# Chunked state-space scan on one core: the state product placed behind the D products, and two low-part subtractions on VectorE instead of GpSimd

## The chip, the cores and the metric

The kernel runs on one core of one Trainium2 chip. The metric is the device time of one execution in microseconds, and less is better. The kernel before takes 2060.54 us, the median of three runs (2057.94, 2060.54 and 2061.54 us).

## What is computed

One layer of a streaming encoder over 1024 tokens of width 1024, in float32: RMSNorm, a mixer of two branches (a gated linear recurrence, and a Mamba-2 state-space scan), a gated merge, an output projection with residual, then RMSNorm, SwiGLU with residual, and a last RMSNorm. The change touches the state-space scan alone. Cut to what matters (heads in 4 groups of 8, head width 64, state 128):

```python
def ssd_scan(x, dt, A, Bm, Cm):
    xdt = (x * dt[..., None])
    a_cs = jnp.cumsum(dt * A, axis=2)                      # within a chunk
    decay = jnp.exp(where(causal, a_cs_l - a_cs_s, -inf))
    scores = einsum('bclgn,bcsgn->bclsg', Cc, Bc)
    y_diag = einsum('bclsg,bclsgk,bcsgkp->bclgkp', scores, decay, xdt)
    decay_to_end = jnp.exp(a_cs[:, :, -1:] - a_cs)
    states = einsum('bclgn,bclgk,bclgkp->bcgkpn', Bc, decay_to_end, xdt)
    # h[c+1] = h[c] * exp(a_cs[c, -1]) + states[c]
    y_off = einsum('bclgn,bcgkpn,bclgk->bclgkp', Cc, prev, jnp.exp(a_cs))
    return y_diag + y_off
# then y + D*x, times silu(z), a group norm, and the branch's weights
```

## The kernel before

The kernel goes through its stages one after the other: first norm and input projections, the recurrence, the scan, the branch weights, the merge and output projection, then the feed-forward part. Most products are in "f32r" with three terms: an operand is split into a high part (a copy by ScalarE) and a low part (the operand less its high part, one subtraction), and high×high, high×low and low×high are added up in one PSUM bank.

The scan runs over 4 head groups and in each over 8 chunks of 128 tokens, 32 chunks in all. For each chunk:

- `chunk_in` (lines 784 to 813): TensorE computes the scores of the chunk and the transpose of B into one "aux" bank (L790, L792), and the transposes of x into the bank "turn" (L795). VectorE makes `xdt` (L802). GpSimd weights it by the decay to the chunk's end, `xwf` (L806); ScalarE copies the high part into `xw` (L808); **GpSimd makes the low part (L809)**. VectorE also makes `xd`, D times x (L811), and multiplies the decays `ed` by the scores (L812).
- `gate_z` (L145): 24 products of z for a chunk further on, which depend on nothing in the scan. They need a free bank among 4 ("mm"), which a SiLU on ScalarE (L772) empties.
- `chunk_out` (from L816): `py`, the old state's part of y, 3 products (L825, from `state_hl`); **`pst`, the state's product, 3 products (L829, from `b_tm` and `xw`)**; **`pd`, the D products, one for each of 8 heads (L832, from `ed` and `xdt`; each shows as two records in the profile)**. Then GpSimd decays the old state (L840), VectorE adds the new part (L841), ScalarE copies its high part (L843) and **GpSimd makes its low part `state_hl` (L844)** for the next chunk's `py`. VectorE scales `py` into `yo` (L848), GpSimd adds it to `xd` (L850), VectorE adds `pd` (L851), GpSimd multiplies by SiLU(z) (L853), ScalarE squares for the norm (L854).
- `chunk_ed` prepares the decays of a later chunk: a load (L778), a subtraction on VectorE (L779), a mask on GpSimd (L781), an exponential on ScalarE (L903).

Four PSUM banks go to z, one to the transposes of x, and three ("aux") are handed round among the scores, `py`, `pst` and `pd`, in the order in which the code asks for them. At the borders between groups VectorE also splits the next group's weights `wz` (L83), four 128x1024 subtractions, and computes a small reciprocal root (L163 to L174).

The order in which each engine's instructions stand is not that of the code: the kernel is built under a scheduler (the last lines of the file ask for it) that reorders instructions by its own estimates. So a change of two lines and one moved block gives a new order on all five engines, and the order is fixed at build: an engine does not pass over an instruction that waits.

Of the kernel before, what the change touches and what calls it, by code (L numbers as in the profile page):

```python
# [13 lines left out]
ALU = mybir.AluOpType  # L14
# [8 lines left out]
HG = 8  # L23
# [9 lines left out]
def hybrid_block_kernel(  # L33
# [6 lines left out]
    nc = tc.nc  # L40
    x, out = x[0], out[0]
# [18 lines left out]
    def bank(tag="aux"):  # L60
        t = psum.tile([P, 512], F32, name=tag, tag=tag, bufs=BANKS[tag])
        return t

    def f32(t):
        return t.bitcast(F32)
# [91 lines left out]
    def flat(t):  # L157
        return t.rearrange("p a b -> p (a b)")
# [50 lines left out]
    def evac(hi, lo, pv):  # L209
        nc.scalar.copy(out=hi, in_=pv)  # L210
        nc.vector.tensor_tensor(out=lo, in0=pv, in1=f32(hi), op=ALU.subtract)
# [496 lines left out]
    with phase("ssd") as pp:  # L708
# [76 lines left out]
        def chunk_in(g, c, b_ch, c_ch, xs_ch, ed):  # L785
            h0 = g * HG
            hs = slice(h0, h0 + HG)
            cs = slice(c * P, (c + 1) * P)
            pt = bank()
            nc.tensor.matmul(pt[:, :P], b_ch[:, cs], c_ch[:, cs], start=True, stop=True)  # L790
            if c < NC - 1:
                nc.tensor.transpose(out=pt[:, P:2 * P], in_=b_ch[:, cs], identity=ident)  # L792
            px = bank("turn")
            for i in range(4):
                nc.tensor.transpose(out=px[:, i * P:(i + 1) * P], in_=xs_ch[i][:, cs], identity=ident)  # L795
            b_tm = None
            if c < NC - 1:
                b_tm = pp.tile([P, 2, P], F32R, name="b_tm", tag="b_tm", bufs=1)
                evac(b_tm[:, 0, :], b_tm[:, 1, :], pt[:, P:2 * P])
            pxv = px.rearrange("p (h d) -> p h d", d=64)  # L800
            xdt = pp.tile([P, HG, 64], F32, name="xdt", tag="xdt", bufs=2)
            nc.vector.tensor_tensor(out=xdt, in0=pxv, in1=bcast(dt_t[:, c, hs], 64), op=ALU.mult)  # L802
            xw = None
            if c < NC - 1:
                xwf = pp.tile([P, HG, 64], F32, name="xwf", tag="tmp", bufs=1)
                nc.gpsimd.tensor_tensor(out=xwf, in0=xdt, in1=bcast(dte_t[:, c, hs], 64), op=ALU.mult)  # L806
                xw = pp.tile([P, 2, GC], F32R, name="xw", tag="xw", bufs=1)
                nc.scalar.copy(out=xw[:, 0, :], in_=flat(xwf))  # L808
                nc.gpsimd.tensor_tensor(out=xw[:, 1, :], in0=flat(xwf), in1=f32(xw[:, 0, :]), op=ALU.subtract)  # L809
            xd = pp.tile([P, HG, 64], F32, name="xd", tag="xd", bufs=3)  # L810
            nc.vector.tensor_tensor(out=xd, in0=pxv, in1=bcast(d_bc[:, hs], 64), op=ALU.mult)  # L811
            nc.vector.tensor_tensor(out=ed, in0=ed, in1=pt[:, :P].unsqueeze(1).broadcast_to([P, HG, P]), op=ALU.mult)  # L812
            return ed, xdt, xw, xd, b_tm
# [3 lines left out]
        def chunk_out(g, c, c_hl, parts, state, sz):  # L817
            ed, xdt, xw, xd, b_tm = parts
# [3 lines left out]
            if c > 0:  # L822
                py = bank()
                for q, (i, j) in enumerate(((0, 0), (0, 1), (1, 0))):
                    nc.tensor.matmul(py, c_hl[:, i, cs], state[1][:, j, :], start=(q == 0), stop=(q == 2))  # L825
            if c < NC - 1:
                pst = bank()
                for q, (i, j) in enumerate(((0, 0), (0, 1), (1, 0))):
                    nc.tensor.matmul(pst, b_tm[:, i, :], xw[:, j, :], start=(q == 0), stop=(q == 2))  # L829
            pd = bank()  # L830
            for h in range(HG):
                nc.tensor.matmul(pd[:, h * 64:(h + 1) * 64], ed[:, h, :], xdt[:, h, :], start=True, stop=True)  # L832
            if c < NC - 1:
                psv = pst.rearrange("p (h d) -> p h d", d=64)
                if c == 0:
                    new = pp.tile([P, HG, 64], F32, name="state", tag="state", bufs=1)
                    nc.vector.tensor_copy(out=new, in_=psv)
                else:
                    new = state[0]
                    nc.gpsimd.tensor_tensor(out=new, in0=new, in1=bcast(dec_t[:, c, hs], 64), op=ALU.mult)  # L840
                    nc.vector.tensor_tensor(out=new, in0=psv, in1=new, op=ALU.add)  # L841
                parts = pp.tile([P, 2, GC], F32R, name="state_hl", tag="state_hl", bufs=1)
                nc.scalar.copy(out=parts[:, 0, :], in_=flat(new))  # L843
                nc.gpsimd.tensor_tensor(out=parts[:, 1, :], in0=flat(new), in1=f32(parts[:, 0, :]), op=ALU.subtract)  # L844
                state = new, parts
            if c > 0:
                yo = pp.tile([P, HG, 64], F32, name="yo", tag="tmp", bufs=1)
                nc.vector.tensor_tensor(out=yo, in0=py.rearrange("p (h d) -> p h d", d=64),  # L848
                                        in1=bcast(eacs_t[:, c, hs], 64), op=ALU.mult)
# [29 lines left out]
        for g in range(NG):  # L879
# [11 lines left out]
            for c in range(NC):  # L891
                parts = chunk_in(g, c, b_ch, c_ch, xs_ch, eds.pop(0))
# [399 lines left out]
    with phase("ffn_out", "right") as pp:  # L1292
# [3 lines left out]
        for f0, nk, wf in pieces:  # L1296
            last = f0 + nk == NFT
            for c in range(NC):
# [22 lines left out]
                if last:  # L1321
# [4 lines left out]
                    for n in range(2):  # L1326
# [3 lines left out]
                        else:  # L1330
                            nc.vector.scalar_tensor_tensor(out=o[:, ns], in0=hres[c][:, ns], scalar=r[:, 0:1],
                                                           in1=g_bc[:, ns], op0=ALU.mult, op1=ALU.mult)
# [33 lines left out]
```

## Time and profile before

| what | us |
|---|---|
| median of three runs | 2060.54 |
| the profiled execution, its own time | 2063.49 |
| its span, from first to last instruction | 2061.7 |
| the window of the scan, 685 to 1030 us of the span | 345 |
| TensorE busy in that window | 316.25 |
| VectorE busy | 251.35 |
| GpSimd busy | 268.50 |
| ScalarE busy | 210.50 |

PE is TensorE's products, PEld its weight loads (they overlap with products), DVE is VectorE, ACT ScalarE, POOL GpSimd, SP the engine that issues most DMAs. "busy" is the time in which an instruction of that engine was under way. On VectorE and GpSimd it includes time in which the instruction has started and is held up by the other of the two. PEclk is the granted TensorE clock as a share of full speed. The profiled execution is 2.95 us above the median.

### The profile page before, as it was taken

Reading aid. Unit: us, or ns where it says so; the run is one execution under the profiler, and the core shown is the slowest. Engines: PE = TensorE matmul, PEld = TensorE weight load, DVE = VectorE, ACT = ScalarE, POOL = GpSimd, SP = SyncE. Lnnn points to the kernel's source line nnn. Section 1 sums busy time; section 2 is a strip of 40 time slices with the busy share of each in tenths; the row PEclk is TensorE's granted clock in tenths of the full one; section 3 lists DMA queues with packets and bytes.
Section 4 is the critical chain, followed back from the end, with each engine's and each line's share of the span. In section 5 each row is a group of like instructions: output and inputs, shape, how many; then the busy total and the mean of one; then the engine's idle time right before and its main releaser. Section 6 shows DMA issues by size and latency. Waiting matters only on the chain.

```text
span 2061.7 us, 23665 instructions
## 1 busy us (share of the span) xinstructions
PE 1975.0 (96%) x8972; PEld 1625.1 (79%) x8972; DVE 1300.8 (63%) x1600; ACT 933.3 (45%) x1329; POOL 721.0 (35%) x470
## 2 busy tenths in 40 slices
PE   5999999999999998998899999998999999999998
PEld 4777877878787887877688888876888888888887
DVE  7787877866675667777546455468555545545445
ACT  5555465567776556666322213334333233342112
POOL 4554544420010688787600030026433433213000
PEclk9999999999999999998899999999999999999999
DMA  5534443442212543442233253521232232255212
GB/s 171 148 104 117 124 122 107 123 133 64 62 54 82 199 144 108 165 157 92 77 103 122 94 172 114 204 82 62 72 103 75 75 96 82 82 186 192 82 62 82
DMA packets 201558, 231.57 MB, mean 112 GB/s; under 512 B 11148, under 2 KB 154980, under 8 KB 201444
## 3 DMA queue, kind: packets, MB, share of 16 engines
q1 hardware_dynamic: 201444, 230.06, 34.8%
q8 instruction: 71, 1.16, 0.2%
q14 instruction: 43, 0.35, 0.1%
HBM read 174.32 MB, written 55.71 MB: 112 GB/s over the span
## 4 chain that ended last, share of the span: by engine, by line
PE 76%; DVE 10%; ACT 4%; POOL 4%; issue 3%; DMA 2%; SPq 0%; DVEq 0%; POOLq 0%; ACTq 0%
PE mm L315 32%; PE mm L134 17%; PE mm L145 15%; PE aux L145 6%; DVE conv L444 2%; DVE wc L83 2%; PE aux L832 2%; DMA w_raw<-in_w_in_dram 1%; POOL xd L853 1%; PE aux L677 1%; POOL xw L809 1%; PE aux L829 1%; POOL state_hl L844 1%; DVE slot L1167 1%; POOL xwf L806 1%
## 5 line engine op out<-in xcount | busy, mean ns | idle before, releaser
L315 PE MATMUL mm<-slot,wc 128*128 128x512 f32 x2376 | 552.9, 391 | 6.1 <-DVE slot L1167 5.0
L315 PEld LDWEIGHTS mm<-slot,wc 128*128 128x128 f32 x2376 | 447.5, 189 | 102.9 <-DVE slot L1167 6.3
L315 PE MATMUL mm<-t,wc 128*128 128x512 f32 x960 | 230.4, 396 | 11.5 <-DVE rows L469 10.0
L315 PEld LDWEIGHTS mm<-t,wc 128*128 128x128 f32 x960 | 182.7, 191 | 53.1 <-DVE rows L469 12.6
L134 PE MATMUL mm<-slot,w_hi 128*128 128x512 f32 x704 | 218.1, 390 | 0.0
L145 PE MATMUL mm<-slot,slot 128*128 128x512 f32 (+1 forms) x924 | 213.0, 387 | 0.0
L145 PE MATMUL mm<-wz,slot 128*128 128x512 f32 x768 | 200.3, 407 | 5.8 <-ACT sz L772 3.8
L145 PEld LDWEIGHTS mm<-slot,slot 128*128 128x128 f32 x924 | 171.6, 188 | 34.9
L83 DVE TENSOR_TENSOR wc<-s,wc 128x512 fp32r<-128x512 f32 x168 | 168.6, 1033 | 32.8 <-ACT wc L82 32.8
L145 PEld LDWEIGHTS mm<-wz,slot 128*128 128x128 f32 x768 | 143.8, 193 | 37.3 <-ACT sz L772 4.7
L134 PEld LDWEIGHTS mm<-slot,w_hi 128*128 128x128 f32 x704 | 132.0, 188 | 27.9 <-DVE dt_rows L617 0.3
L134 PE MATMUL mm<-slot,w_lo 128*128 128x512 f32 x352 | 137.1, 389 | 0.0
L145 PE MATMUL aux<-slot,slot 128*128 128x512 f32 x528 | 124.4, 389 | 0.0
L444 DVE SCALAR_TENSOR_TENSOR conv<-rows,par,conv 128x1023 f32<-128x1023 f32 (+2 forms) x72 | 115.4, 1607 | 4.6 <-ACT conv L440 4.5
L145 PEld LDWEIGHTS aux<-slot,slot 128*128 128x128 f32 x528 | 99.1, 188 | 20.6
L1103 POOL TENSOR_TENSOR u_u<-u_u,e 128x512 f32<-128x512 f32 x22 | 28.6, 1300 | 246.0 <-DVE u_u L1097 246.0
L82 ACT CAST slot<-w_raw 128x1024 fp32r<-128x1024 f32 x44 | 46.0, 1052 | 141.3 <-PE mm L145 52.6
L82 ACT CAST wc<-s 128x512 fp32r<-128x512 f32 x168 | 98.0, 617 | 10.6 <-POOL s L430 4.8
L82 ACT CAST w_hi<-w_raw 128x1024 fp32r<-128x1024 f32 x36 | 37.7, 1050 | 136.2 <-PE mm L134 133.3
L488 POOL TENSOR_TENSOR rows<-rows,e 128x512 f32<-128x512 f32 x20 | 41.3, 2067 | 162.9 <-DVE rows L477 95.0
L83 DVE TENSOR_TENSOR slot<-w_raw,slot 128x1024 fp32r<-128x1024 f32 x44 | 57.4, 1310 | 52.4 <-ACT slot L82 52.3
L982 POOL TENSOR_TENSOR acc<-acc,gt 128x1024 f32<-128x1024 f32 x8 | 20.6, 2583 | 187.9 <-DMA gt<-g_dram 187.9
(291 smaller groups left out, 3535.8 us busy)
## 6 DMA issues: line engine op xcount, KB each, us to landing
w_raw<-in_w_in_dram SPq DMA_DIRECT2D x60, 512.0 KB, 4.6
ed<-acs_dram SPq DMA_DIRECT2D x32, 512.0 KB, 3.8
xbc_dram<-conv SPq DMA_DIRECT2D x24, 512.0 KB, 2.7
w_raw<-in_w_branch_dram SPq DMA_DIRECT2D x24, 512.0 KB, 3.6
w_raw<-in_w_ffn_in_dram SPq DMA_DIRECT2D x22, 512.0 KB, 4.4
raw_pair<-in_w_ffn_in_dram SPq DMA_DIRECT2D x22, 512.0 KB, 4.5
act_dram<-act SPq DMA_DIRECT2D x22, 512.0 KB, 2.7
act_raw<-act_dram SPq DMA_DIRECT2D x22, 512.0 KB, 3.5
```

Of the source, the lines that this page charges most:

```text
L82: nc.scalar.copy(out=hi, in_=src)
L83: nc.vector.tensor_tensor(out=lo, in0=src, in1=f32(hi), op=ALU.subtract)
L134: nc.tensor.matmul(ps[:m, :], ww[:, k, :], xx(p, k, h), start=(k == 0 and i == 0), stop=(k == nk - 1 and i == 2))
L145: nc.tensor.matmul(ps, xx(p, k), ww(q, k), start=(k == 0 and i == 0), stop=(k == nk - 1 and i == 2))
L315: nc.tensor.matmul(ps, w[:, k, :], x[q][:, k, :], start=(start and k == 0 and i == 0), stop=(k == 3 and i == 2), skip_group_check=True)
L444: nc.vector.scalar_tensor_tensor(out=t[:, d:], in0=x[:, :S - d], scalar=tap[j], in1=t[:, d:], op0=ALU.mult, op1=ALU.add)
L488: nc.gpsimd.tensor_tensor(out=d["hi"][:, half(1)], in0=d["hi"][:, half(1)], in1=d["e5"], op=ALU.add)
L677: nc.tensor.matmul(pg, w[:, j, :], uu[:, hs], start=(q == 0), stop=(q == 2))
L806: nc.gpsimd.tensor_tensor(out=xwf, in0=xdt, in1=bcast(dte_t[:, c, hs], 64), op=ALU.mult)
L809: nc.gpsimd.tensor_tensor(out=xw[:, 1, :], in0=flat(xwf), in1=f32(xw[:, 0, :]), op=ALU.subtract)
L832: nc.tensor.matmul(pd[:, h * 64:(h + 1) * 64], ed[:, h, :], xdt[:, h, :], start=True, stop=True)
L1103: nc.gpsimd.tensor_tensor(out=d["u3"], in0=d["u3"], in1=d["e5"], op=ALU.add)
```

## The change

In `chunk_in` the low part of `xw` and in `chunk_out` the low part of `state_hl` are computed by VectorE instead of GpSimd: same operands, same shape (128x512, float32 from SBUF in, f32r out). In `chunk_out` the block that issues `pd` stands ahead of the one that issues `pst`. The products are the same ones. Line numbers of the changed file differ in two places: there the D products are L828 and the state product is L832.

```diff
                 nc.scalar.copy(out=xw[:, 0, :], in_=flat(xwf))
-                nc.gpsimd.tensor_tensor(out=xw[:, 1, :], in0=flat(xwf), in1=f32(xw[:, 0, :]), op=ALU.subtract)
+                nc.vector.tensor_tensor(out=xw[:, 1, :], in0=flat(xwf), in1=f32(xw[:, 0, :]), op=ALU.subtract)
...
+            pd = bank()
+            for h in range(HG):
+                nc.tensor.matmul(pd[:, h * 64:(h + 1) * 64], ed[:, h, :], xdt[:, h, :], start=True, stop=True)
             if c < NC - 1:
                 pst = bank()
                 for q, (i, j) in enumerate(((0, 0), (0, 1), (1, 0))):
                     nc.tensor.matmul(pst, b_tm[:, i, :], xw[:, j, :], start=(q == 0), stop=(q == 2))
-            pd = bank()
-            for h in range(HG):
-                nc.tensor.matmul(pd[:, h * 64:(h + 1) * 64], ed[:, h, :], xdt[:, h, :], start=True, stop=True)
...
                 nc.scalar.copy(out=parts[:, 0, :], in_=flat(new))
-                nc.gpsimd.tensor_tensor(out=parts[:, 1, :], in0=flat(new), in1=f32(parts[:, 0, :]), op=ALU.subtract)
+                nc.vector.tensor_tensor(out=parts[:, 1, :], in0=flat(new), in1=f32(parts[:, 0, :]), op=ALU.subtract)
```

What the scheduler makes of it, at two places. First TensorE, at a chunk in the middle of a group, before (`turn` holds the transposes of x; `xw`, `b_tm` go into the state product, `xdt`, `ed` into the D products):

```order
L795 MATMUL turn<-ident,xs_6200 128x128
L829 MATMUL aux<-xw,b_tm 128x512 x3
L832 MATMUL aux<-xdt,ed 128x64 x8
L790 MATMUL aux<-c_ch,b_ch 128x128
L792 MATMUL aux<-ident,b_ch 128x128
```

and in the changed kernel, at a chunk of the same kind:

```order
L795 MATMUL turn<-ident,xs_5501 128x128
L825 MATMUL aux<-state_hl,c_hl 128x512
L828 MATMUL aux<-xdt,ed 128x64 x8
L832 MATMUL aux<-xw,b_tm 128x512 x3
```

What was the transposes, the state product, the D products is now the transposes, the old state's product, the D products, the state product. At 28 of the 32 chunks there is a state product, and in the changed order it never stands ahead of all D products of its chunk.

Second VectorE, one chunk in the middle of the third group, before:

```order
L211 TENSOR_TENSOR b_tm<-aux,b_tm 128x128
L812 TENSOR_TENSOR ed<-ed,aux 128x1024
L779 TENSOR_TENSOR ed<-ed,acs_t 128x1024
L848 TENSOR_TENSOR yo<-aux,eacs_t 128x512
L841 TENSOR_TENSOR state<-aux,state 128x512
L851 TENSOR_TENSOR xd<-aux,xd 128x512
L802 TENSOR_TENSOR xdt<-turn,dt_t 128x512
L811 TENSOR_TENSOR xd<-turn,d_bc 128x512
```

and in the changed kernel:

```order
L211 TENSOR_TENSOR b_tm<-aux,b_tm 128x128
L812 TENSOR_TENSOR ed<-ed,aux 128x1024
L848 TENSOR_TENSOR yo<-aux,eacs_t 128x512
L851 TENSOR_TENSOR xd<-aux,xd 128x512
L802 TENSOR_TENSOR xdt<-turn,dt_t 128x512
L811 TENSOR_TENSOR xd<-turn,d_bc 128x512
L841 TENSOR_TENSOR state<-aux,state 128x512
L211 TENSOR_TENSOR b_tm<-aux,b_tm 128x128
L812 TENSOR_TENSOR ed<-ed,aux 128x1024
L809 TENSOR_TENSOR xw<-xwf,xw 128x512
L779 TENSOR_TENSOR ed<-ed,acs_t 128x1024
L844 TENSOR_TENSOR state_hl<-state,state_hl 128x512
```

The two subtractions (L809, L844) have joined VectorE's queue, and the addition of the state (L841), which stood between `yo` and the addition of `pd` (L851), now stands behind the next chunk's `xdt` and `xd`: L851 follows L848 directly. On GpSimd 28 instructions of L809 and 28 of L844 are gone from the queue. In SP's queue the loads of `ed` and the stores of `y_dram` change places with each other and with some loads. Outside the scan the orders are the same.

## Rows read from the trace of the kernel before

**Rows 1.** The page, its span and part 1.

```profile
span 2061.7 us, 23665 instructions
PE 1975.0 (96%) x8972; PEld 1625.1 (79%) x8972; DVE 1300.8 (63%) x1600; ACT 933.3 (45%) x1329; POOL 721.0 (35%) x470
```

**Rows 2.** Busy time by engine, the window of the scan; columns in the first row.

```profile
core 0: us, PE busy (x) PEld busy (x) DVE busy (x) ACT busy (x) POOL busy (x), PEclk, DMA share, GB/s
685.00:1030.00 345.00, 316.25 (x1644) 263.50 (x1643) 251.35 (x330) 210.50 (x298) 268.50 (x200) 0.93 0.38 126
```

**Rows 3.** The same view by stretches of 20 us, four of them.

```profile
780.00:800.00 20.00, 15.84 (x79) 11.80 (x79) 17.64 (x24) 12.65 (x18) 17.02 (x12) 1.00 0.53 159
...
820.00:840.00 20.00, 20.00 (x113) 17.09 (x112) 11.21 (x15) 14.14 (x20) 17.96 (x15) 1.00 0.51 184
...
860.00:880.00 20.00, 16.57 (x81) 12.76 (x80) 19.08 (x30) 13.67 (x18) 14.57 (x11) 0.97 0.46 145
...
1000.00:1020.00 20.00, 14.89 (x58) 11.62 (x57) 9.62 (x13) 4.52 (x9) 12.19 (x11) 0.66 0.17 53
```

**Rows 4.** PE's groups, 680 to 1030 us: busy, mean, idle before, releasers.

```profile
L145 PE MATMUL mm<-wz,slot 128*128 128x512 f32 x663 | 175.7, 409 | 5.8 <-ACT sz L772 3.8 <-DVE wz L83 1.1 <-ACT wz L82 0.9
...
L829 PE MATMUL aux<-xw,b_tm 128*128 128x512 f32 x84 | 32.8, 452 | 9.9 <-ACT xw L808 6.0 <-POOL xw L809 3.8
L825 PE MATMUL aux<-state_hl,c_hl 128*128 128x512 f32 x84 | 31.8, 435 | 3.5 <-ACT state_hl L843 2.6 <-POOL state_hl L844 0.8
```

**Rows 5.** PE in order of time, the five longest waits of the state product.

```profile
798.96 0.73 PE L829 MATMUL aux<-xw,b_tm 128*128 128x512 f32 x2 [2.28 <-POOL xw L809]
...
878.26 0.50 PE L829 MATMUL aux<-xw,b_tm 128*128 128x512 f32 x1 [1.98 <-ACT xw L808]
...
963.27 0.50 PE L829 MATMUL aux<-xw,b_tm 128*128 128x512 f32 x1 [2.30 <-ACT xw L808]
...
997.76 0.72 PE L829 MATMUL aux<-xw,b_tm 128*128 128x512 f32 x2 [0.95 <-POOL xw L809]
...
1005.39 0.80 PE L829 MATMUL aux<-xw,b_tm 128*128 128x512 f32 x1 [1.15 <-ACT xw L808]
```

**Rows 6.** DVE in order of time, the decay products of the same five chunks.

```profile
796.68 1.21 DVE L812 TENSOR_TENSOR ed<-ed,aux 128x1024 f32<-128x1024 f32 x1
...
879.24 1.20 DVE L812 TENSOR_TENSOR ed<-ed,aux 128x1024 f32<-128x1024 f32 x1
...
959.83 1.21 DVE L812 TENSOR_TENSOR ed<-ed,aux 128x1024 f32<-128x1024 f32 x1
...
996.70 1.20 DVE L812 TENSOR_TENSOR ed<-ed,aux 128x1024 f32<-128x1024 f32 x1
...
1003.41 1.21 DVE L812 TENSOR_TENSOR ed<-ed,aux 128x1024 f32<-128x1024 f32 x1
```

**Rows 7.** POOL's groups of the two moved subtractions, 680 to 1030 us.

```profile
L809 POOL TENSOR_TENSOR xw<-xwf,xw 128x512 fp32r<-128x512 f32 x28 | 41.5, 1482 | 7.8 <-ACT xw L808 7.8
...
L844 POOL TENSOR_TENSOR state_hl<-state,state_hl 128x512 fp32r<-128x512 f32 x28 | 39.0, 1392 | 19.5 <-ACT state_hl L843 19.4
```

**Rows 8.** DVE subtractions out of SBUF, ns min/median/max: other stages, then the scan.

```profile
L83 DVE TENSOR_TENSOR wc<-s,wc x168: 671/686/1784, 86.8 to 1797.1; 128x512 fp32r<-128x512 f32 x168
...
L779 DVE TENSOR_TENSOR ed<-ed,acs_t x32: 1207/1717/2305, 683.5 to 995.1; 128x1024 f32<-128x1024 f32 x32
```

**Rows 9.** DVE and POOL in order of time, around 818 us.

```profile
817.75 2.01 DVE L779 TENSOR_TENSOR ed<-ed,acs_t 128x1024 f32<-128x1024 f32 x1
...
817.38 1.30 POOL L809 TENSOR_TENSOR xw<-xwf,xw 128x512 fp32r<-128x512 f32 x1
818.63 2.04 POOL L840 TENSOR_TENSOR state<-state,dec_t 128x512 f32<-128x512 f32 x1
```

**Rows 10.** PE in order of time: the 16 records of D products, two chunks.

```profile
989.61 1.89 PE L832 MATMUL aux<-xdt,ed 128*128 128x64 f32 x16
...
1005.98 3.51 PE L832 MATMUL aux<-xdt,ed 128*128 128x64 f32 x16
```

**Rows 11.** Waits, 680 to 1030 us: total, times, longest.

```profile
ACT sz L854 <- POOL xd L853: 50.8, 26, 6.8
```

## The prediction, written before the changed kernel ran

> **What bounds the kernel now.** I read the page first: TensorE is busy 1975.0 of 2061.7 us [rows 1], so the kernel can gain only where TensorE idles or runs slowly. The order of every engine outside the scan is unchanged, so the window of the scan alone counts. There TensorE is busy 316.25 of 345 us, which leaves 28.75 us of idle time, at a mean granted clock of 0.93 [rows 2]. The other engines come next: GpSimd 268.50, VectorE 251.35 us, 78% and 73% of the window. By stretches [rows 3], the middle of a group (820 to 840 us) has no idle TensorE at all; the borders between groups lose 4.16 us (780 to 800) and 3.43 us (860 to 880), and there VectorE is busy 17.64 and 19.08 of 20 us; near the end, where no z products are left to fill with, 5.11 us are lost (1000 to 1020).
>
> The groups of TensorE say who ends the idle time [rows 4]: the state product waits 9.9 us for the two parts of `xw`, the z products 5.8 us, mostly for the SiLU that empties their bank, and the old state's product 3.5 us for `state_hl`. These are what the change can reach.
>
> **What moves off GpSimd.** 28 + 28 subtractions, 41.5 + 39.0 = 80.5 us of its busy time, a mean of 1.44 us each [rows 7]. GpSimd falls to about 188 us, 54% of the window.
>
> **What that costs on VectorE.** The same shape out of SBUF takes 0.671 us at best, 0.686 at the median and 1.784 at worst in other stages [rows 8]. Why it varies is plain from one place [rows 9]: VectorE's subtraction starts at 817.75, GpSimd's instruction ends at 818.68, and the 2.01 us are that wait and a bare 1.207 us [rows 8]; GpSimd's next one, begun at 818.63, then takes 2.04 us, as it is held until VectorE ends at 819.76. They exclude each other. Bounds: 56 × 0.671 = 37.6 us and 56 × 1.784 = 99.9 us. I take the nearest row, the scan's own L779: its median is 0.51 us above its minimum while GpSimd is 78% busy; at 54% that is 0.51 × 54/78 = 0.35 us. So 0.686 + 0.35 = 1.04 us each, 58.3 us in all, and L779 itself gains 32 × 0.16 = 5 us. VectorE comes to 251.4 + 58.3 − 5 = 305 us, 88% of the window, and becomes as full as TensorE.
>
> The Trainium skill (GPSIMD Engine Reference, Engine selection) sends elementwise work to VectorE, since GpSimd is about twice as slow with two inputs. Undisturbed durations agree (0.686 [rows 8] against 1.30 us [rows 9]), but by it alone VectorE would get 56 × 0.686 = 38 us and end at 285; the scan's own row says 305, and I go by that row.
>
> **Term 1: the state product's waits, −4.7 us.** The D products now stand first. Their operands decide how much sooner TensorE goes on: the decay product L812 of the same chunk [rows 5, 6]. The stall that ended at 798.96 began at 796.68; L812 ended at 797.89, so 1.07 us are won. The one ending at 963.27: L812 ended 961.04, 2.23 us won. The one at 1005.39: L812 ended 1004.62, 0.77 us. At 997.76 it ended 997.90 and nothing is won; at 878.26 it ended 2.2 us later than the state product started, nothing again. That is 4.1 of the 8.66 us of the five; of the other 1.2 us I take half. Bounds: 0 (VectorE later by its new work) and −9.9. The D products then cover `xw`'s low part: 16 records take 1.89 us at full speed [rows 10].
>
> **Term 2: z products, −1.9 us.** ScalarE stands 50.8 us before its square, waiting for GpSimd's multiplication [rows 11], and the SiLU that frees z's bank is queued behind that square. GpSimd has 30% less to do. I take half of the 3.8 us [rows 4]; bounds 0 and −3.8.
>
> **Term 3: the slow clock, −2.4 us.** After stalls the same D products take 3.51 instead of 1.89 us [rows 10], in a stretch with a granted clock of 0.66 [rows 3], that is partly at 1.2 instead of 2.4 GHz. One and a half of the five stalls go; at 1.6 us each −2.4. Bounds 0 and −8.
>
> **Term 4: VectorE's lateness, +3.1 us.** Its new work takes up 53 of its 94 idle us. Mid-group, z products cover that. At a border VectorE is already at 19.08 of 20 us [rows 3], and every instruction added in front of `xdt` or the decay product reaches TensorE. I take one on the path at each of three borders, 3 × 1.04; bounds 0 and both subtractions of two chunks at each, 12 × 1.04 = 12.5.
>
> At nothing I cost: the state product itself (same products, later by the D products; the state's low part is needed only by the next chunk, and mid-group 24 z products lie between); the aux banks (the old state's product now takes the bank that `pd` leaves, not that of `pst`; mid-group it comes a chunk of z later); ScalarE (61% busy); SP's loads of `ed`, whose buffers come free sooner, as D products read them. If the z products run out, as after 1000 us, each of these shows; that is the second rival.
>
> **Sum.** −4.7 − 1.9 − 2.4 + 3.1 = −5.9, against the profiled execution's own 2063.49 us: 2057.6. That run stands 2.95 above the median, so for the median 2054.6; I say 2054.5, with 2049 to 2058 as this case's own range (a term 1 of nearly all 9.9, or a term 4 twice as large).
>
> **Rivals.**
>
> *VectorE becomes the bound at the borders (slower).* The place is the 3 group borders, the price term 4's upper bound of 12.5 us with term 1 still won: 2060.5 + 12.5 − 4.7 = 2068. It decides once the two subtractions of a border's chunks find no gap, which is where VectorE has less than 2 us free in 20. For it: 19.08 and 17.64 of 20 already [rows 3], and L851 now directly behind L848, with a GpSimd addition between them to wait for. Against: waits for GpSimd are a part of that busy time, and they shrink. Chance 0.25. The Trainium skill (SBUF — State Buffer, "two separate sides") states that VectorE with two SBUF inputs and GpSimd take their shared port as an exclusive lock for a whole instruction; rows 9 agree. By its worst case each moved subtraction waits out a whole GpSimd instruction, about the 1.784 us bound above.
>
> *The wait only changes its name (no change).* Three of the five stalls have the decay product as late as `xw` [rows 5, 6], and the old state's product (3.5 us of waits [rows 4]) now gets `state_hl` later: the state product starts up to 1.89 us later, the subtraction is shorter by only 0.4. Four such waits at +1.5 are 6 us, which cancels the sum: 2060.5. Chance 0.26.
>
> *The two engines stop holding each other up (much faster).* GpSimd's chain paced the borders and the end, and all of 9.9 + 3.8 + 3.5 us goes, with a part of the slow clock: 2060.5 − 17.2 − 2.4 = 2041. For it: mid-group GpSimd is busy 17.96 of 20 us. Against: rows 6. Chance 0.12.
>
> That the change is not made is no rival: the orders show all 56 moved.
>
> **How the numbers follow.** The forecast has 0.37, the rivals 0.25, 0.26 and 0.12. A difference counts above 0.2%, about 4.1 us, the least that a measurement of this kernel can tell: faster is below 2056.4, slower above 2064.7. Of the forecast 0.03 lies within 0.2%, of the no-change case 0.01 above: faster 0.37 − 0.03 + 0.12 = 0.46, same 0.26 + 0.03 − 0.01 = 0.28, slower 0.26. The range 2043 to 2069 leaves out half of the much-faster case and the worst of the slow one.
>
> **What would show it.** Right, if in the new profile the state product's idle time is under 2 us, GpSimd's busy time in the scan near 188 us and VectorE's near 305, the subtractions at a mean near 1.04 us, and TensorE's idle time in the scan near 22 us. Wrong, if the D products or the score products (L790) have taken over those waits, named by VectorE; or if VectorE is above 19 us in the 20-us stretches at the borders and the scan is longer than before.

## The result and the profile after

The changed kernel takes 2089.47 us, median of 4 runs (2088.91 to 2093.54); the kernel before, on the same chip, takes 2061.04 us (4 runs). The ratio is 1.0138, 95% interval 1.0119 to 1.0158: **slower by about 28 us**, where 6 us faster was forecast, and outside the range. The profiled execution of the changed kernel took 2089.79 us.

The page, its span and part 1, against [rows 1]:

```profile
span 2088.0 us, 23654 instructions
PE 1988.9 (95%) x8972; PEld 1634.7 (78%) x8972; DVE 1324.8 (63%) x1656; ACT 921.1 (44%) x1319; POOL 643.6 (31%) x414
```

The span grew by 26.3 us. TensorE has the same 8972 products, in 13.9 us more, and 12.4 us more of idle time. The records of one line in order of time tell where; here the D products of the last part of the scan (number, ns shortest/median/longest, start of the first and of the last), of the kernel before:

```profile
L832 PE MATMUL aux<-xdt,ed x96: 217/416/422, 963.6 to 1016.6; 128*128 128x64 f32 x96
```

and of the changed one:

```profile
L828 PE MATMUL aux<-xdt,ed x144: 217/275/472, 963.5 to 1043.5; 128*128 128x64 f32 x144
```

The last D product starts 26.9 us later, so the scan holds the whole difference. With 16 records for a chunk, the kernel before has 6 chunks to go at 963 us and the changed one 9: the loss is spread over the scan. Its window, against [rows 2], ends here at 1055 us:

```profile
core 0: us, PE busy (x) PEld busy (x) DVE busy (x) ACT busy (x) POOL busy (x), PEclk, DMA share, GB/s
685.00:1055.00 370.00, 326.32 (x1635) 269.59 (x1634) 274.86 (x382) 196.76 (x286) 189.94 (x144) 0.90 0.36 117
```

TensorE idles 43.7 us instead of 28.75 and works at a mean granted clock of 0.90 instead of 0.93; its busy time there is 326.32 instead of 316.25 us, 10 us more for about the same products. VectorE is busy 74% of the window: it did not become full. TensorE's groups, against [rows 4]:

```profile
L145 PE MATMUL mm<-wz,slot 128*128 128x512 f32 x660 | 176.1, 415 | 9.0 <-ACT sz L772 6.1 <-DVE wz L83 2.2 <-ACT wz L82 0.7
L828 PE MATMUL aux<-xdt,ed 128*128 128x64 f32 x512 | 72.2, 300 | 9.4 <-DVE ed L812 9.3
L825 PE MATMUL aux<-state_hl,c_hl 128*128 128x512 f32 x84 | 33.9, 459 | 15.1 <-ACT state_hl L843 9.9 <-DVE state_hl L844 4.9
L832 PE MATMUL aux<-xw,b_tm 128*128 128x512 f32 x84 | 31.1, 471 | 0.0
```

The state product's 9.9 us are gone to the last tenth (the forecast: under 2 us left). In their place the **old state's product** (L825) waits 15.1 instead of 3.5 us, for the two parts of `state_hl` that the state product leads to, and the D products wait 9.3 us for the decay product of VectorE, one of the prediction's own signs of being wrong. On VectorE the moved subtractions and their neighbours:

```profile
L809 DVE TENSOR_TENSOR xw<-xwf,xw 128x512 fp32r<-128x512 f32 x28 | 27.0, 965 | 1.1 <-ACT xw L808 1.1
L844 DVE TENSOR_TENSOR state_hl<-state,state_hl 128x512 fp32r<-128x512 f32 x28 | 25.3, 905 | 2.3 <-ACT state_hl L843 2.3
L802 DVE TENSOR_TENSOR xdt<-turn,dt_t 128x512 f32<-128x512 f32 x32 | 21.8, 683 | 14.7 <-PE aux L828 14.0 <-PE turn L795 0.3
L851 DVE TENSOR_TENSOR xd<-aux,xd 128x512 f32<-128x512 f32 x32 | 21.8, 682 | 18.1 <-PE aux L828 16.7 <-POOL xd L850 1.4
...
L848 DVE TENSOR_TENSOR yo<-aux,eacs_t 128x512 f32<-128x512 f32 x28 | 19.2, 684 | 22.9 <-PE aux L825 22.8
```

In the last three of these lines VectorE stands 22.8 + 16.7 + 14.0 = 53.5 us waiting for TensorE. In the same three of the kernel before it was 9.5 + 2.9 + 2.4 = 14.8 us (the addition of the state, L841, waited another 7.6 us there, 1.4 now):

```profile
L848 DVE TENSOR_TENSOR yo<-aux,eacs_t 128x512 f32<-128x512 f32 x28 | 19.2, 686 | 29.4 <-POOL xw L809 9.9 <-PE aux L825 9.5 <-issue 8.7
L851 DVE TENSOR_TENSOR xd<-aux,xd 128x512 f32<-128x512 f32 x32 | 22.0, 686 | 12.2 <-POOL xd L850 8.7 <-PE aux L832 2.9
L802 DVE TENSOR_TENSOR xdt<-turn,dt_t 128x512 f32<-128x512 f32 x32 | 21.8, 681 | 3.5 <-PE aux L832 2.4 <-PE turn L795 1.1
```

TensorE does not lose its time where VectorE is full. By stretches of 20 us, in the changed kernel, the one with the busiest VectorE (19.79 us) costs TensorE 0.11 us, and in the one in which TensorE loses most, 6.47 us, VectorE is busy 11.99 us:

```profile
780.00:800.00 20.00, 19.89 (x118) 17.10 (x118) 19.79 (x34) 14.66 (x21) 8.69 (x6) 1.00 0.46 149
```

```profile
880.00:900.00 20.00, 13.53 (x58) 10.42 (x58) 11.99 (x15) 8.58 (x13) 6.03 (x5) 0.83 0.43 142
```

This second stretch shows how both engines come to wait for each other. TensorE in order of time (start, duration, in brackets the idle time ahead and who ended it):

```profile
884.26 0.80 PE L825 MATMUL aux<-state_hl,c_hl 128*128 128x512 f32 x1 [2.86 <-ACT state_hl L843]
886.17 6.73 PE L145 MATMUL mm<-wz,slot 128*128 128x512 f32 x19 [1.11 <-ACT sz L772]
892.74 1.89 PE L828 MATMUL aux<-xdt,ed 128*128 128x64 f32 x16
894.44 0.71 PE L825 MATMUL aux<-state_hl,c_hl 128*128 128x512 f32 x2
894.99 0.86 PE L832 MATMUL aux<-xw,b_tm 128*128 128x512 f32 x3
895.68 1.33 PE L145 MATMUL mm<-wz,slot 128*128 128x512 f32 x5
...
900.77 1.07 PE L825 MATMUL aux<-state_hl,c_hl 128*128 128x512 f32 x2 [2.36 <-DVE state_hl L844]
```

and VectorE in the same stretch, then ScalarE's copy of the state:

```profile
886.48 1.57 DVE L844 TENSOR_TENSOR state_hl<-state,state_hl 128x512 fp32r<-128x512 f32 x1
894.67 0.69 DVE L802 TENSOR_TENSOR xdt<-turn,dt_t 128x512 f32<-128x512 f32 x1 [6.61 <-PE aux L828]
...
896.47 0.68 DVE L841 TENSOR_TENSOR state<-aux,state 128x512 f32<-128x512 f32 x1
898.54 1.57 DVE L779 TENSOR_TENSOR ed<-ed,acs_t 128x1024 f32<-128x1024 f32 x1 [1.39 <-DMA ed<-acs_dram]
900.04 0.68 DVE L844 TENSOR_TENSOR state_hl<-state,state_hl 128x512 fp32r<-128x512 f32 x1
```

```profile
897.24 0.62 ACT L843 CAST state_hl<-state 128x512 fp32r<-128x512 f32 x1 [8.63 <-DVE state L841]
```

From the end of the state product (895.85) to the old state's product that needs its low part (900.77) there are 4.9 us: the addition, ScalarE's copy (done at 897.86), and the subtraction, which starts only at 900.04, as it stands in VectorE's queue behind an L779 that waits for its load. Five z products and a few small ones cover half of that. The other 19 z products stand ahead of the D products. The low part of the older state was ready at 888.05 (L844, 886.48 + 1.57), so most of their 6.73 us covers nothing, and there VectorE waits 6.61 us for the buffer of `xdt` that the D products read. The Trainium skill (PSUM — Partial Sum Buffer, Engine vs sequencer instructions) states that matrix products start and complete in program order and that VectorE's queue is strictly first in, first out. Both listings agree: L844 at 900.04 behind L779, and the two old state's products at 894.44, behind z and D products though their operand had been ready since 888.05.

The whole scan shows the same. Of the waits of the old state's product that the listing of the changed kernel names one by one (14.9 us), 8.9 us fall where 10 or fewer z products stand between the state product and it, 3.7 us in the last chunks, which have no z products, and 2.3 us elsewhere. In the kernel before all of them (3.4 us) fall in the last chunks.

### The profile page after: what moved, and what is told of

It reads as the page before. It is cut to its first block, busy times and chain, and to the rows that moved or that the text cites. A ratio compares the mean times of both kernels' runs of the same rounds, so it can differ in the third digit from the quotient of the medians.

```text
span 2088.0 us, 23654 instructions
## 1 busy us (share of the span) xinstructions
PE 1988.9 (95%) x8972; PEld 1634.7 (78%) x8972; DVE 1324.8 (63%) x1656; ACT 921.1 (44%) x1319; POOL 643.6 (31%) x414
## 4 chain that ended last, share of the span: by engine, by line
PE 48%; DVE 2%; DMA 0%; ACT 0%; issue 0%; POOL 0%; DVEq 0%; ACTq 0%; POOLq 0%
PE mm L315 19%; PE mm L134 12%; PE mm L145 10%; PE aux L145 6%; DVE slot L1167 1%; PE aux L740 0%; DMA v_raw<-y_dram 0%; PE aux L828 0%; PE aux L206 0%; DVE t L1156 0%; DVE wc L83 0%; DVE o L1331 0%; DVE xb L1152 0%; DVE xb L1158 0%; POOL ed L781 0%
## 5 line engine op out<-in xcount | busy, mean ns | idle before, releaser
L145 PEld LDWEIGHTS mm<-wz,slot 128*128 128x128 f32 x768 | 149.3, 199 | 43.4 <-ACT sz L772 8.2
L828 PEld LDWEIGHTS aux<-xdt,ed 128*128 128x128 f32 x512 | 71.8, 217 | 15.9 <-DVE ed L812 10.8
```

The lines of the kernel that those rows point to most:

```text
L145: nc.tensor.matmul(ps, xx(p, k), ww(q, k), start=(k == 0 and i == 0), stop=(k == nk - 1 and i == 2))
```

## Experiments

Two theories to begin with: the loss is the new order of the D products and the state product (A in the expectations), or it is VectorE's new load (B); C is that only both together cost it. Of the order it could be the places that the scheduler chose for the z products (A1), the state that reaches the next old state's product late (A2, later A2a), or the single buffers of `xw` and `b_tm`, held longer (A2b). All ratios are to the kernel before, measured again beside each group of runs (its medians there are 2059.4 to 2062.7 us), with their 95% intervals.

**The parts alone.** r_only has the block of D products ahead and leaves both low parts on GpSimd. xs has both low parts on VectorE and the old order; x_only and s_only move one of the two.

```diff
-                nc.gpsimd.tensor_tensor(out=xw[:, 1, :], in0=flat(xwf), in1=f32(xw[:, 0, :]), op=ALU.subtract)
+                nc.vector.tensor_tensor(out=xw[:, 1, :], in0=flat(xwf), in1=f32(xw[:, 0, :]), op=ALU.subtract)
...
-                nc.gpsimd.tensor_tensor(out=parts[:, 1, :], in0=flat(new), in1=f32(parts[:, 0, :]), op=ALU.subtract)
+                nc.vector.tensor_tensor(out=parts[:, 1, :], in0=flat(new), in1=f32(parts[:, 0, :]), op=ALU.subtract)
```

(the two edits of xs; the first alone is x_only, the second alone s_only)

> Only the D products stand ahead of the state product; both low parts stay on GpSimd. Theory A (the order on TensorE did it: the state comes later, and the z products collect in long rows between the scan's steps, so that VectorE's queue stands behind a D product or an old-state product): most of the 28 us are here, 2080 to 2092 us, with VectorE waiting for TensorE's products (L848, L851, L802) 40 us or more in the scan instead of 15. Theory B (VectorE's two new subtractions did it): 2055 to 2067 us. Theory C (only both together): within 8 us of before.

> Only the two low parts are on VectorE; the state product stands ahead of the D products as before. Theory A: 2050 to 2066 us, the state product's wait of 9.9 us smaller. Theory B: 2080 to 2092 us, with VectorE above 19 us of 20 at the borders. Theory C: within 8 us of before.

> Only the low part of the weighted inputs is on VectorE. Theory A: 2052 to 2064 us. Theory B: about half of the 28 us, 2070 to 2080 us, if both subtractions count alike.

> Only the low part of the state is on VectorE. Theory A: 2052 to 2064 us. Theory B: about half of the 28 us, 2070 to 2080 us, if both subtractions count alike; more than the weighted inputs' low part if VectorE's queue makes the state late, since the old state's product waits for it.

Measured: r_only 2099.02 us, 1.018 (1.0163 to 1.0197); xs 2046.64, 0.9927 (0.9912 to 0.9941); x_only 2053.86, 0.9957 (0.9944 to 0.997); s_only 2045.19, **0.9915 (0.9899 to 0.9931), the lowest of all**, though not clear of xs. A had the directions right and some sizes wrong (r_only 7 us above its range, xs and s_only 3 and 7 us below, x_only inside); B's ranges are missed by 16 us or more each time, and C falls with r_only and xs. The window of the scan in xs:

```profile
685.00:1030.00 345.00, 324.51 (x1709) 272.29 (x1709) 287.67 (x390) 215.63 (x306) 190.29 (x144) 0.94 0.40 131
```

VectorE is fuller here than in the changed kernel (83% against 74%), and this kernel is 15 us faster than the one before. VectorE's load as the cause has fallen; the order alone costs about 37 us, and the low parts give about 10 to 15 back. In r_only VectorE waits for TensorE 33.8 + 7.3 + 7.3 = 48.4 us at L851, L848 and L802, without any new work of its own. TensorE's waits in r_only:

```profile
L825 PE MATMUL aux<-state_hl,c_hl 128*128 128x512 f32 x84 | 34.5, 467 | 16.8 <-ACT state_hl L843 8.7 <-POOL state_hl L844 8.1
L832 PE MATMUL aux<-xw,b_tm 128*128 128x512 f32 x84 | 34.4, 512 | 15.0 <-ACT xw L808 12.1 <-POOL xw L809 2.9
```

**The order of TensorE held fixed.** To move one thing only, TensorE's order in the scan was written out as a string and laid on with edges that fix the order of issue and nothing else: z products, S scores, B transpose of B, X transposes of x, Y old state's, T state's, D D products, with a count behind each.

```diff
+        ORDER = "z102SBz3Xz6Xz7Xz7Xz26X4z3Tz2D3T2D5SBX4z16Yz2T3z4Y2D8X..."
+        chain = [made[k].pop(0) for k, n in re.findall(r"([A-Za-z])(\d*)", ORDER) for _ in range(int(n or 1))]
+        for a, b in zip(chain, chain[1:]):
+            tc.add_manual_dep(b, a.name, mybir.DependencyInfo(mybir.DependencyClass.NoSync, mybir.DependencyReason.DATA), reason="order")
```

pin_same writes out the order of the kernel before, unchanged (the control). pin_late has each chunk's T behind its last D, and no z product moved. pin_rows is r_only's order with T back ahead of D. after_xsrows has the three edits of the change, with the order of xs but for T, which stands behind D. pin_late and after_xsrows, and the kernels late_... further down, also have the change's order in the code, so that D asks for its bank ahead of T.

```diff
 pin_same to pin_late, one chunk
-D2Y2D6z10SBz2YzY2X4z11T3D8
+D2Y2D6T3z10SBz2YzY2X4z11D8T3
```

> The kernel before, with the order of the scan's products on TensorE written out as it stands there: a control for the next ones. Every theory: within 6 us of before.

> The order on TensorE is that of the kernel before, z products where they were, and only each chunk's three state products are moved behind the last of its D products; low parts on GpSimd. Theory A1 (the new places of the z products cost the time: they collect in rows between the steps of the scan): 2055 to 2072 us. Theory A2 (the later state itself costs it): 2085 to 2102 us, with the old state's product waiting 15 us or more.

> The order on TensorE is that of the kernel with only the D products ahead (2099 us), z products where they are there, but each chunk's three state products stand ahead of its D products again; low parts on GpSimd. Theory A1: 2085 to 2102 us. Theory A2: 2055 to 2072 us.

> The changed kernel (low parts on VectorE, D products ahead of the state product), with the z products in the places that they have in the kernel with the low parts alone (2047 us). Theory A1: 2042 to 2060 us. Theory A2: 2075 to 2092 us.

Measured: pin_same 2066.98 us, 1.0025 (1.0013 to 1.0037); pin_late 2079.61, 1.0082 (1.0067 to 1.0097); pin_rows 2156.54, 1.0453 (1.0436 to 1.0471); after_xsrows 2096.66, 1.0161 (1.0146 to 1.0176). pin_late lies between the ranges of A1 and A2, with the wait that A2 named; pin_rows and after_xsrows lie above both of theirs, so neither theory came out whole. The control costs 6 us, as the other engines' queues are laid out anew under a fixed TensorE, so these kernels are compared with pin_same. With no z product moved, T behind D costs 12.6 us, and the wait is at the old state's product. pin_same, then pin_late:

```profile
L837 PE MATMUL aux<-xw,b_tm 128*128 128x512 f32 x84 | 33.0, 456 | 13.8 <-ACT xw L816 9.1 <-POOL xw L817 4.5
L833 PE MATMUL aux<-state_hl,c_hl 128*128 128x512 f32 x84 | 32.3, 440 | 3.5 <-ACT state_hl L851 2.1 <-DVE yo L856 1.2 <-POOL state_hl L852 0.2
```

```profile
L833 PE MATMUL aux<-state_hl,c_hl 128*128 128x512 f32 x84 | 35.1, 475 | 21.4 <-POOL state_hl L852 12.6 <-ACT state_hl L851 7.5 <-DMA ed<-acs_dram 0.9
L840 PE MATMUL aux<-xw,b_tm 128*128 128x512 f32 x84 | 28.9, 450 | 1.0 <-POOL xw L817 1.0
```

The state product loses 12.8 us of waits, the old state's gains 17.9. In all, TensorE's idle time between 685 and 1070 us grows by 7.0 us (34.45 to 41.47) of the 10.4 us between the two profiled spans. So the places of the z products are not all of it. Those of the kernel before, given back, take 19.4 us off r_only (pin_late); those of xs take nothing off the changed kernel (after_xsrows). Against xs, after_xsrows is 50.0 us slower (of which some 6 can be the writing out), and the old state's product waits 37.5 us in it instead of 6.0. But T ahead of D is not the better order everywhere: in pin_rows, with the z products as r_only has them, it is 57.5 us slower than r_only, and the z products wait 39.8 us, mostly for the SiLU that frees their bank:

```profile
L774 PE MATMUL mm<-wz,slot 128*128 128x512 f32 x660 | 192.6, 444 | 39.8 <-ACT sz L780 38.8 <-DVE wz L83 0.9
```

**Other remedies, which missed.** after_ylate moves the old state's product behind the D products in the changed kernel, so that its wait would be covered; xs_ylate does the same in xs. after_buf2 and xs_buf2 give `xw` and `b_tm` two buffers each.

```diff
 after_ylate
-            if c > 0:
-                py = bank()
...
             pd = bank()
             for h in range(HG):
                 nc.tensor.matmul(pd[:, h * 64:(h + 1) * 64], ed[:, h, :], xdt[:, h, :], start=True, stop=True)
+            if c > 0:
+                py = bank()
...
 after_buf2, xs_buf2
-                b_tm = pp.tile([P, 2, P], F32R, name="b_tm", tag="b_tm", bufs=1)
+                b_tm = pp.tile([P, 2, P], F32R, name="b_tm", tag="b_tm", bufs=2)
...
-                xw = pp.tile([P, 2, GC], F32R, name="xw", tag="xw", bufs=1)
+                xw = pp.tile([P, 2, GC], F32R, name="xw", tag="xw", bufs=2)
```

> The changed kernel, with the old state's product moved as well: D products, old state's product, state product. The old state's product then asks for the state one row of D products later. Theory A2a (the state comes too late for the next chunk's old-state product, and TensorE stands): 2050 to 2075 us, the wait of that product under 8 us instead of 15. Theory A2b (the weighted inputs `xw` and the transposed B have one buffer each, which the later state product holds longer, so that ScalarE's queue stands): 2080 to 2098 us.

> Low parts on VectorE, state product first as before, and the old state's product behind the D products. Theory A2a: the state is in time there, so nothing is won, 2042 to 2060 us. Theory A2b says the same.

> The changed kernel with two buffers each for `xw` and the transposed B. Theory A2a: 2080 to 2098 us. Theory A2b: 2045 to 2070 us.

> Low parts on VectorE, state product first as before, two buffers for `xw` and the transposed B: a control for the buffers alone. Both theories: within 6 us of 2047.

Measured: after_ylate 2146.57 us, 1.0414 (1.0394 to 1.0434); xs_ylate 2134.53, 1.0355 (1.034 to 1.0371); after_buf2 2098.60, 1.0183 (1.0166 to 1.02); xs_buf2 2052.73, 0.996 (0.9945 to 0.9974). Second buffers make neither faster, and in the changed kernel ScalarE waits only 3.7 us for the buffer of `xw` (L808, for the state product): there the buffers are not the cause. In r_only and pin_late that wait is 19.0 and 20.5 us, and there second buffers were not tried. In after_ylate the old state's product no longer waits at all, but the D products do, for a VectorE that has fallen behind:

```profile
L824 PE MATMUL aux<-xdt,ed 128*128 128x64 f32 x512 | 80.7, 325 | 43.7 <-DVE ed L812 43.7
```

after_ylate and xs_ylate lie more than 70 us above what A2a expected of them (2050 to 2075 and 2042 to 2060). Why these two lose so much was not followed up further; the scheduler laid out every engine anew in both.

**Cover.** What was left to try: between T of one chunk and Y of the next lies the path addition, copy, low part, and whatever TensorE does in between covers it. D behind T was a part of that cover; D ahead of T is none. same_low and late_low are pin_same and pin_late with both low parts on VectorE. late_cover and late_low_cover are pin_late and late_low with Y moved down to stand directly ahead of its own chunk's D, behind that chunk's z products and transposes, except in the last six chunks, which have no z left.

```diff
 pin_late to late_cover, one chunk
-D2Y2D6T3z10SBz2YzY2X4z11D8T3
+D8T3z10SBz3X4z11Y3D8T3
```

> TensorE's order of the kernel before, written out (as in pin_same, 2067 us), with both low parts on VectorE: nothing but the engine of the 56 subtractions differs from pin_same. If the move of the low parts is a gain by itself (shorter subtractions, GpSimd less busy), about 2050 to 2056, the same 10 to 14 us as without the written-out order. If the 14 us of that kernel came from the places that the scheduler then chose for the z products, 2064 to 2069, no difference from pin_same.

> TensorE's order of pin_late (order of the kernel before, state products moved behind the D products, 2079.6 us), with both low parts on VectorE; so with pin_same, pin_late and same_low this is the fourth of a square in which z products never move. If the two parts of the change add up: 2079.6 less what the low parts gain in same_low, some 2066 to 2070. If the late state makes VectorE's new work worse (the subtractions stand in the path from the state product to the next old state's product, on an engine that also waits for the D products), it is no better than pin_late: 2078 to 2090, with the old state's product waiting over 20 us for state_hl.

> As pin_late (2079.6 us, low parts on GpSimd), but where z products are left each old state's product stands directly ahead of its chunk's D products, so that all z products and transposes of the chunk lie between the state product of the chunk before and it; z products keep their places. If what the moved state product loses is cover between it and the next old state's product, that wait falls from 21.4 us to under 8 and the time to 2062 to 2070. If the loss is elsewhere (yo, its addition and the last sum come later and hold the bank of the D products), it stays at 2078 or above, with waits at the D or score products for a bank.

> As late_cover, with both low parts on VectorE: the change's three edits in an order that gives the state all of the cover there is. If cover is what the change lacked, this comes within 4 us of same_low or below it (2048 to 2058). If D products ahead of the state product cost by something else, it stays above 2066.

Measured, with TensorE's order fixed and all z products in the places of the kernel before:

| | low parts on GpSimd | low parts on VectorE |
|---|---|---|
| T ahead of D | pin_same 2066.98 | same_low 2053.77, 0.9975 (0.9959 to 0.999) |
| T behind D | pin_late 2079.61 | late_low 2071.48, 1.0057 (1.004 to 1.0075) |
| T behind D, Y moved down | late_cover 2057.65, 0.9992 (0.9976 to 1.0008) | late_low_cover 2057.71, 0.9986 (0.9969 to 1.0004) |

The move of Y takes 22.0 us off pin_late and 13.8 off late_low. late_low_cover came out as the theory of cover expected (2048 to 2058), late_cover below what it expected (2062 to 2070); late_low lies close above the sum of the two parts (2066 to 2070), though its old state's product waits 21.4 us, as in pin_late. One border chunk shows it; pin_late:

```profile
789.64 0.94 PE L840 MATMUL aux<-xw,b_tm 128*128 128x512 f32 x3
790.42 2.67 PE L774 MATMUL mm<-wz,slot 128*128 128x512 f32 x10
...
798.75 0.80 PE L833 MATMUL aux<-state_hl,c_hl 128*128 128x512 f32 x1 [4.04 <-ACT state_hl L851]
...
804.30 1.22 PE L833 MATMUL aux<-state_hl,c_hl 128*128 128x512 f32 x2 [4.33 <-POOL state_hl L852]
...
806.02 2.14 PE L774 MATMUL mm<-wz,slot 128*128 128x512 f32 x5
```

and late_cover at the same chunk:

```profile
788.15 2.89 PE L774 MATMUL mm<-wz,slot 128*128 128x512 f32 x11 [0.20 <-DVE wz L83]
790.88 0.40 PE L833 MATMUL aux<-state_hl,c_hl 128*128 128x512 f32 x1
793.00 0.74 PE L833 MATMUL aux<-state_hl,c_hl 128*128 128x512 f32 x2 [1.72 <-POOL state_hl L852]
793.58 2.19 PE L836 MATMUL aux<-xdt,ed 128*128 128x64 f32 x16
```

8.37 us of waits became 1.72, with the 24 z products and the transposes now all between T and Y. But the path got shorter too: from the end of T to the start of the last two Y products it takes 13.72 us in pin_late and 9.44 in late_cover. The addition of the state on VectorE (L849) starts 5.71 us after the end of T in the one and 1.73 us after it in the other; pin_late, then late_cover:

```profile
796.29 0.68 DVE L849 TENSOR_TENSOR state<-aux,state 128x512 f32<-128x512 f32 x1
```

```profile
785.29 0.68 DVE L849 TENSOR_TENSOR state<-aux,state 128x512 f32<-128x512 f32 x1
```

Of the 6.65 us won at this chunk, 4.28 are the shorter path and about 2.4 more work between. Over the scan the old state's product waits 9.5 instead of 21.4 us in late_cover (under 8 was expected), and 13.2 instead of late_low's 21.4 in late_low_cover. ScalarE's wait for the buffer of `xw` falls as well, from 20.5 us in pin_late to 3.5 in late_cover. late_low's row, then late_cover's, then late_low_cover's:

```profile
L833 PE MATMUL aux<-state_hl,c_hl 128*128 128x512 f32 x84 | 34.7, 470 | 21.4 <-DVE state_hl L852 15.9 <-ACT state_hl L851 5.1
```

```profile
L833 PE MATMUL aux<-state_hl,c_hl 128*128 128x512 f32 x84 | 31.1, 455 | 9.5 <-POOL state_hl L852 7.3 <-ACT state_hl L851 2.1
```

```profile
L833 PE MATMUL aux<-state_hl,c_hl 128*128 128x512 f32 x84 | 31.3, 458 | 13.2 <-DVE state_hl L852 9.8 <-ACT state_hl L851 3.3
```

**Does the later Y pay by itself?** same_low_cover is same_low, and s_cover is s_only's order written out, both with Y moved down in the same way to stand ahead of T.

```diff
 same_low to same_low_cover, one chunk
-D2Y2D6z10SBz2YzY2X4z11T3D8
+D8z10SBz3X4z11Y3T3D8
```

> As same_low (2053.8 us: TensorE's order of the kernel before, low parts on VectorE, state products ahead of the D products), with each old state's product moved down to stand directly ahead of its own chunk's state product, behind the z products. There the state product of the chunk before already has the D products as cover and the old state's product waits only 3.1 us. If cover is what counts and there is enough, nothing is won: 2050 to 2056. If the move pays by something else, such as the later yo letting VectorE do other work first, it wins 10 us or more as it did in late_cover: under 2046.

> The order of s_only (state first, only the state's low part on VectorE; 2045.2 us, its waits at the old state's product are small), written out, with the old state's product moved down in the same way. Writing out an order alone cost 6 us in pin_same. If the early old state's product costs nothing here: 2045 to 2052. If its move pays by itself: 2035 to 2042, the best of all.

Measured: same_low_cover 2056.88 us, 0.9993 (0.998 to 1.0007), which is 3 us above same_low and just above what was expected without a gain, and s_cover 2048.89, 0.9953 (0.9937 to 0.9968), no better than s_only. Where D already covers the state's path, moving Y down wins nothing. So the 22 and 14 us above are not won by a later Y as such, but only where T stands behind D. That they are cover fits the waits; how much of them is cover, and how much the shorter path and the buffer of `xw`, was not separated.

## Why the prediction was wrong

**The failed step** is the line "At nothing I cost: the state product itself (same products, later by the D products; the state's low part is needed only by the next chunk, and mid-group 24 z products lie between)". Two things in it were wrong. The D products were themselves cover for the path from the state product to the next chunk's old state's product, and the moved block takes them away. And the 24 z products don't all lie between: as seen at 884 to 901 us, 19 stood ahead of the D products and 5 behind the state product. Those 19 took 6.73 us, more than the path's 4.9. In the fixed order the state product behind the D products costs 12.6 us with the low parts on GpSimd and 17.7 with them on VectorE (late_low against same_low), and the wait at the old state's product goes from 3.5 to 21.4 and from 3.1 to 21.4 us.

**The rival that named it was too cheap.** "The wait only changes its name" had the right place, the old state's product, but priced it at four waits of 1.5 us, 6 us, and at no change in sum. It measured 11.6 us more idle time there in the changed kernel (15.1 against 3.5), and what hangs on it was not priced: VectorE held up by TensorE for 53.5 us, 9.3 us of the D products' waiting for VectorE, and the clock, 0.90 instead of 0.93, where Term 3 had forecast a gain. The rival also counts three stalls in which the decay product is as late as `xw`; by the rows that Term 1 works from there are two, at 997.76 and 878.26.

**Term 1** was right as a mechanism and more than right in size: the state product's waits went from 9.9 to 0.0, where −4.7 was the sum's share. Whether the reorder pays when cover is kept is not shown with the low parts on GpSimd: late_cover is 9.3 us below pin_same, but Y moves in it too, and that move with T ahead of D was not run there. With the low parts on VectorE it was run, and the reorder wins nothing (late_low_cover 2057.71, same_low_cover 2056.88, same_low 2053.77); the state product's waits had already fallen from 13.8 to 7.0 us in same_low.

**Term 2** fell: the z products wait 9.0 us, not less than 5.8, with SiLU still the main cause. **Term 4** and the rival of a full VectorE fell too: its busy time is 74% of the window, and kernels with more of it are faster. Two stretches of 20 us do stand above 19 us, as its sign said (19.79 from 780 us, 19.05 from 960), but TensorE loses only 0.11 and 1.50 us in them. What VectorE's queue did cost is one instruction behind another that waits, as L844 behind L779, not its load.

**The prices of the move** held roughly. GpSimd was forecast at 188 us and is at 189.94. The 56 subtractions took (27.0 + 25.3) / 56 = 0.93 us each, not 1.04. In rows 9 the wait and the bare time give 0.93 + 1.207 = 2.14 us, not quite the 2.01 of the row; the price does not hang on it, as it was taken from medians and minima. The Trainium skill (GPSIMD Engine Reference, Engine selection) sends elementwise work with two inputs to VectorE. xs, the kernel in which only that was done, is faster, which agrees. With the undisturbed 0.686 us the prediction estimated that VectorE would end at 285 us; xs shows 287.67, closer than the 305 that I took from the scan's own row. What was missing was the gain: the low parts on VectorE are worth 13 us with TensorE's order fixed (same_low against pin_same) and 15 us in xs, and I had entered them mostly as a cost.

**What stays open.** The change's own order is 18.0 us slower than late_low, and r_only's 19.4 us slower than pin_late, though the edits are the same: there the scheduler also chose new places for the z products, and with them new queues on the other engines. That these places matter pin_rows shows; what of them cost the 18 us was not separated, nor why the order of xs with T behind D loses 50.0 us. More cover was tried in written-out orders only; a like move of Y left to the scheduler (after_ylate) lost another 57 us.

## What to carry to other kernels

Before a block moves past another on an in-order engine, ask what it was covering: take the path that starts at the instruction behind it (here the state's product, addition, copy, low part), measure its length in the trace, and count the work left between it and its next reader. The path's length is not fixed either: it holds the queues of every engine on it. A wait that disappears at the moved instruction says nothing about the sum; the reader at the other end of the path has to be priced too. Where a scheduler lays out the code, a moved block is a new order on all engines: write the old order out, move one thing, and compare with a written-out control.

## What the runs showed that was not expected

The size of it: the same products in other orders, with the low parts on one engine or the other, spread over 2045 to 2157 us. And the price of a stall goes on after it: in pin_late five z products took 2.14 us behind the two waits at 806 us, where ten took 2.67 us at 790 us, in a stretch (785 to 810 us) whose mean granted clock was 0.80. From 785 to 790 us, with TensorE busy throughout, it was 1.00; from 798 to 805 us, after 8 us in which TensorE was busy 4.15, it was 0.50, which is 1.2 instead of 2.4 GHz:

```profile
785.00:810.00 25.00, 16.07 (x75) 12.30 (x74) 20.06 (x23) 14.70 (x18) 19.25 (x13) 0.80 0.40 120
```

In late_cover the same 25 us show 23.07 us of busy TensorE at 0.93. One edit out of the three, s_only, beats both kernels: the state's low part alone on VectorE, 2045.19 us.
